# Depthwise convolutions: from 31 taps on GpSimd to block-diagonal products on TensorE

## The chip, the cores and the metric

The kernel runs on one core of a Trainium2 chip. The core has five engines that work at the same time, each through its own queue of instructions: TensorE (PE: matrix products; its weight loads are listed as PEld), VectorE (DVE), ScalarE (ACT), GpSimd (POOL) and SyncE (SP), which here only issues transfers (DMAs). The metric is the time of one execution on the device, in microseconds (us). Products write to PSUM, everything else lies in SBUF, 128 partitions each; weights and inputs come from DRAM.

## The reference, cut to what matters

Two blocks follow each other on one sequence of 256 tokens of 1024 features. The first is a state-space mixer with a squared-ReLU network. The second has two layers with two streams, the tokens x and a context ctx of 256 tokens. In each layer a stream is normalised, multiplied by w_in and split into parts for four branches (Fourier, convolution, grouped attention, differential attention), whose gated sum is multiplied by w_out; a SwiGLU network follows. In the second layer the context only gives keys and values. The branch that matters here:

```python
def conformer_conv(z, w, bias, ln_g, ln_b):          # z [256 tokens, 1024]
    a, g = jnp.split(z, 2, axis=-1)
    u = a * jax.nn.sigmoid(g)                          # [256, 512]
    pad = CONV_KERNEL // 2                             # 15; CONV_KERNEL = 31
    y = lax.conv_general_dilated(u, w[:, None, :].astype(u.dtype), window_strides=(1,),
                                 padding=[(pad, pad)], dimension_numbers=("NWC", "WIO", "NWC"),
                                 feature_group_count=CONV_WIDTH_2) + bias
    return jax.nn.silu(layer_norm(y, ln_g, ln_b))

def mixer_stream(parts, lp, cos, sin, ctx_kv, lam, lam_init):
    zf, zconv, zgq, zgk, zgv, zdq, zdk, zdv, zgate = parts
    y_four = fourier_mix(zf) @ lp["w_four"]
    y_conv = conformer_conv(zconv, lp["conv_w"], lp["conv_b"], ...) @ lp["w_conv"]
    ...                                                # the two attentions
    ys = jnp.stack([y_four, y_conv, y_gqa, y_diff], axis=2)
    return jnp.sum(gates * ys, axis=2) @ lp["w_out"]
```

Every one of the 512 channels has its own 31 taps, so y at token t is the sum over i of w[i] times u at token t + i - 15. It is computed three times: for ctx and x in layer 0, and for x in layer 1.

## The kernel before, in words

Activations lie as [features on partitions, 256 tokens], in chunks of 128 features. A large product is made in three passes of a rounded 32-bit type: weight and activation are each split into a high part and the rest, and high times high, high times rest and rest times high are summed (mm3, L337; token-major products do the same at L992 to L994). A weight unit of 512 KB is loaded by SP's queue into a ring of three buffers (ws), rounded by ScalarE (wh, L315) and its rest taken by VectorE (wl, L316), each into a ring of four. So a product waits for a load, ScalarE and VectorE in turn, and loads wait in SP's one queue, in order.

A convolution call (conv_start, L1417) has two parts. conv_in (L998) makes four chunks of 128 channels: two weight units, 48 products, a tanh on ScalarE (L1009) and a product on VectorE (L1010) that writes 2u into up, [128, 4, 286], with 15 zeros on each side of the tokens. conv_taps (L1013) works on GpSimd alone: for a chunk, tap 0 times up and the bias, then 30 times a multiplication into ct (L1025) and an addition to cy (L1026), each of 128x256. cy is read only much later, by conv_steps (L1029: layer norm and silu), beside the last gated branches. The three calls stand at L1653 (ctx, layer 0, inside the end of block 1), L1665 (x, layer 0) and L1693 (x, layer 1).

What follows a call on TensorE are the token-major products of keys, values and queries (w_tok), with their rotations on VectorE and their transposes (L1205), the attentions (softmax at L1249 to L1254; transposes at L1262; values) with Fourier and gated branches between their steps, and then the rest of the branches. RMS norms sum squares (ssq, L413), add over partitions on TensorE (L388), take 1/sqrt on VectorE by steps on columns of one or two elements (L366 to L381) and spread the row by a diagonal matrix dg (L396) and a product (L397).

The order on each engine is set when the program is built, by a scheduler that follows priorities (the order of the code, with shifts) and the rings of buffers: tiles of one tag and lane share as many buffers as BUFS gives, and a new tile waits for the last reader of an old one. The tag px of the main lane, small results in PSUM, has two. Modulation vectors are made in block 1 by float32 products with a stationary of 128x32, four of them on the four groups of 32 output rows (L902).

Of the kernel before, what the change touches and what calls it, by code (L numbers as in the profile page):

```python
# [9 lines left out]
F32 = mybir.dt.float32  # L10
# [7 lines left out]
P = 128  # L18
D = 1024
L = 256  # L20
# [7 lines left out]
# columns of the packed per-feature vector array  # L28
# [3 lines left out]
def _vec_layout():  # L32
    off = 0
    for name, n in (
        ("norm_ffn", 8), ("norm_ple", 8), ("norm_final", 8), ("final_norm", 8),
        ("norm_mix2", 16), ("norm_ffn2", 16), ("b_ada", 96), ("c", 16),
        ("conv_b", 8), ("ln_g", 8), ("ln_b", 8), ("diff_norm", 2), ("conv_w", 248),
        ("lam", 512), ("qn", 128), ("kn", 128),
    ):
        VEC[name] = (off, n)  # L40
        off += n
    return off
# [21 lines left out]
# ---------------------------------------------------------------- host layout  # L64
# [4 lines left out]
def _wfeat(w, cols_per_unit=1):  # L69
    """[K, M] -> [M/128 blocks][128, K/128, 128]."""  # L70
    k, m = w.shape
    return w.reshape(k // P, P, m // P, P).transpose(2, 1, 0, 3)


def host_layout(i):
# [5 lines left out]
    # rows (s, h), columns (g, c); token = 8c + s  # L81
# [22 lines left out]
    put("conv_w", a["conv_w_2"].reshape(2, 31, 4, P).transpose(3, 0, 2, 1).reshape(P, 248))  # L104
    lam = np.stack([a["lam_q1_2"], a["lam_k1_2"], a["lam_q2_2"], a["lam_k2_2"]], axis=1)
    put("lam", np.broadcast_to(lam.reshape(1, 512), (P, 512)))
# [10 lines left out]
    # group g = (half*4 + g4)*8 + j ; rows (half, p), columns (j, g4)  # L117
# [10 lines left out]
    # rows (re/im, p), columns (half, j, g4, h); then the same with re and im exchanged  # L128
# [12 lines left out]
    # block 1 weights  # L141
# [11 lines left out]
    # block 2 weights  # L153
    w_in = a["w_in_2"]
    # [l, 2048 columns, half, k] of [128, 4 * 256]: a quarter's columns side by side
# [5 lines left out]
    o["w_cin"] = np.stack(wc).reshape(8, P, 2048)  # L161
    tok = np.concatenate([w_in[:, :, 0:512], w_in[:, :, 1536:3840]], axis=2)
# [17 lines left out]
    for l in range(2):  # L180
        w = _wfeat(a["w_ffn2_2"][l])  # [8, 128, 22, 128]
# [7 lines left out]
    # constants of the shapes  # L189
# [18 lines left out]
    rope = np.stack([np.cos(ra), np.sin(ra)], axis=1)  # [256, 2, 32]  # L208
# [10 lines left out]
# ---------------------------------------------------------------- device side  # L219
class Act:  # L220
    """A [features, tokens] activation as hi/lo float32r tiles of 4 KB per partition."""
# [21 lines left out]
    def pair(self, k):  # L243
        """hi and lo of chunks k, k + 1 (both in one tile)."""
        i = k % self.per
        return self._tile(0, k)[:, i : i + 2, :], self._tile(1, k)[:, i : i + 2, :]


# buffers per tag and lane: m main, a attention and modulation vectors, c convolution, g gates
# [13 lines left out]
class Net:  # L263
# [7 lines left out]
    # ---- tiles  # L271
# [5 lines left out]
    def lane(self, s):  # L277
        """Tiles of one lane take turns among themselves, so lanes can run past each other."""
# [34 lines left out]
    # ---- hi/lo parts: hi is rounded to float32r, lo is the exact remainder  # L313
# [4 lines left out]
    def split_scaled(self, hi, lo, src, c):  # L318
        """hi + lo = c * src, c a constant or a column."""
# [3 lines left out]
    # ---- weights  # L323
    def wunits(self, ap, sizes=(1024, 1024)):
        """Load one weight chunk; return its units as (hi, lo) pairs."""
# [11 lines left out]
    def mm3(self, out, unit, act, ks, off=0, start=True, stop=True, cols=None):  # L337
        """out += unit[:, off + 128*i].T @ act[:, k] over ks, in three float32r passes."""
# [12 lines left out]
    def mm3x(self, outs, units, act, n=KC):  # L351
        """Several units over n chunks of act, chunk by chunk as act comes."""
# [7 lines left out]
    # ---- norms  # L360
    def newton(self, v, n):
        """1/sqrt(v) for v > 0, v in SBUF, [128, n]."""
# [21 lines left out]
    def colsum(self, out, ssq):  # L384
        """Sum of the tiles [128, 256] over partitions; the tokens land on the partitions of out [128, 2]."""
# [5 lines left out]
    def bcast(self, y):  # L391
        """[128 tok, 2] -> PSUM [128, 256]: the row of tokens on every partition."""
# [7 lines left out]
    def ssq_add(self, ssq, src, k, n, scale=None, eng=None):  # L400
        """Squares of chunk k of n: the last two stay apart, to be summed by colsum."""
# [17 lines left out]
    # ------------------------------------------------------------ S5  # L419
    def exp_small(self, out, x, n):  # L420
        """exp on a small [128, n] tile with float32 accuracy."""
# [58 lines left out]
    def s5_params(self):  # L480
# [21 lines left out]
        # powers a^(8-i), i = 0..7, [128, 32, 8]  # L502
# [17 lines left out]
        # coef = (a - 1) / lam  # L520
# [15 lines left out]
        # B-bar [128, ri, 32, 16]  # L536
# [12 lines left out]
        # rows (ri, p), columns (half, g): B-bar, zeros, B-bar; and the powers signed for C  # L549
# [13 lines left out]
        # recursion multipliers: [a^8 re | a^8 re], [-a^8 im | a^8 im]  # L563
# [7 lines left out]
    def b_outer(self, dst, g0, xr, xi):  # L571
        """dst[:, g, ri, i, h] = a[g]^(8 - i) * B[g, h]."""
# [15 lines left out]
    def s5(self):  # L588
# [12 lines left out]
        # normalised input, rows (s, h), columns (g, c)  # L601
# [18 lines left out]
        # chunk summaries S = sum_s a^(8-s) B u  # L620
# [7 lines left out]
        for jp in range(4):  # L628
            ss_sb = self.k4([P, 2, 2, 2, 64], F32, "ss")  # (j, ri, half, p) on rows (g4, c)
            for jj in range(2):  # L630
# [3 lines left out]
                pmt = self.k4([P, 4, 2, P], F32, "pmt")  # rows (s, h); (g4, ri, (half, p))  # L634
# [21 lines left out]
        # recursion over chunks  # L656
        for s in range(1, 31):
# [7 lines left out]
            if s in (23, 30):  # L665
                # from rows (half, p), columns (ri, g) to rows (ri, p), columns (half, g)
# [7 lines left out]
        # rows (ri, p): C a^s, minus the imaginary part; order i = 7 - s  # L674
# [9 lines left out]
        # taps K_tau = Re(C a^tau B), order i = 7 - tau; rows (g4, 2, h'), the second half one tap on  # L684
        for half in range(2):
# [15 lines left out]
            # intra-chunk matrices: rows (s', h'), columns (7 - s, h)  # L701
# [10 lines left out]
        # outputs, rows (g4, c); columns (7 - s, j, h)  # L712
# [40 lines left out]
    def c_outer(self, c, g0, c1, c2):  # L753
# [6 lines left out]
        # C conj-signed: re = Cr pr - Ci pi; -im = -Ci pr - Cr pi  # L760
# [6 lines left out]
    # ------------------------------------------------------------ block 1 after the mixer  # L767
    def ple_proj(self):
        """p @ ple_w, two tiles of four feature chunks."""
# [13 lines left out]
    def block1(self, ya, pe, early, fill):  # L783
        V, G, S, T, nc = self.V, self.G, self.S, self.T, self.nc
        x = self.x
        # gated linear unit, residual, first norm
# [20 lines left out]
        # squared-relu network; the row scale 1/rms enters squared, on its output  # L807
# [42 lines left out]
        # gated addition of p; the final norm and the next block's first norm  # L850
# [30 lines left out]
    # ------------------------------------------------------------ modulation vectors  # L881
    def silu_c(self):
        """silu of c and c_ctx as [128, k, 32] stationary columns, zero beyond the two."""
# [9 lines left out]
    def ada_steps(self, g):  # L893
        """Layer 0: modulation columns of 2048 features, silu(c) W, a quarter of them on each 32 rows."""
# [24 lines left out]
    def ada_late(self):  # L919
        """Layer 1: the products on the vector engine, their sums over the partitions on the tensor engine;  # L920
        each 32 rows carry 512 features of one of the two streams."""
# [30 lines left out]
    def ada_next(self, n=1):  # L952
        """Some steps of the modulation vectors left, beside other work."""
# [4 lines left out]
    def mod_gain(self, l, kind, norm):  # L958
        """norm * (1 + scale) as columns [128, 8, 2]."""
# [21 lines left out]
    # ------------------------------------------------------------ mixers  # L981
    def tok_seg(self, h, units):
        """[128 tok, 2, 256] = h[:, token blocks].T @ W from token-major weight units of four k;
        a generator, one step per token block."""
# [13 lines left out]
    def conv_in(self, l, h):  # L998
        V, S, G = self.V, self.S, self.G
        up = self.up.tile([P, 4, L + 30], F32, tag="up", name=self.nm("up"))  # L1000
        G.memset(up[:, :, 0:15], 0.0)
        G.memset(up[:, :, L + 15 : L + 30], 0.0)
# [732 lines left out]
```

## Time and profile before

| | |
|---|---|
| runs of the kernel | 2120.98, 2123.73 and 2126.22 us, median 2123.73 |
| profiled execution, span from first to last instruction | 2118.8 us |
| TensorE busy | 1945.7 us, 92% of the span |
| VectorE busy | 1582.7 us, 75% |
| ScalarE busy | 928.6 us, 44% |
| GpSimd busy | 773.5 us, 37% |

The time of an execution is the span and a little around it, which the profile doesn't list; the span shown stands 4.9 us under the median. The profile is one execution. A group of instructions is told by its line, engine and operation, then out<-in by the program's names and the shapes; "busy, mean ns of one" and the idle time of the engine before them follow. A window's row gives the busy time and number of instructions of PE, PEld, DVE, ACT and POOL, in this order, in a stretch, and the granted clock of TensorE as a share of full speed. A mean over the span hides that stages have different limits, so the rows further down go by stretch.

### The profile page before, as it was taken

Reading aid. Unit: us, or ns where it says so; the run is one execution under the profiler, and the core shown is the slowest. Engines: PE = TensorE matmul, PEld = TensorE weight load, DVE = VectorE, ACT = ScalarE, POOL = GpSimd, SP = SyncE. Lnnn points to the kernel's source line nnn. Section 1 sums busy time; section 2 is a strip of 40 time slices with the busy share of each in tenths; the row PEclk is TensorE's granted clock in tenths of the full one; section 3 lists DMA queues with packets and bytes.
Section 4 is the critical chain, followed back from the end, with each engine's and each line's share of the span. In section 5 each row is a group of like instructions: output and inputs, shape, how many; then the busy total and the mean of one; then the engine's idle time right before and its main releaser. Section 6 shows DMA issues by size and latency. Waiting matters only on the chain. (4 is left out here: it accounts for less than half of the span.)

```text
span 2118.8 us, 39621 instructions
## 1 busy us (share of the span) xinstructions
PE 1945.7 (92%) x15666; PEld 1811.3 (85%) x15666; DVE 1582.7 (75%) x2761; ACT 928.6 (44%) x1583; POOL 773.5 (37%) x882
## 2 busy tenths in 40 slices
PE   3869999986999997898999999999997899999998
PEld 1457999985789996777999989989997778999997
DVE  9974686779687779879868766675769887766665
ACT  2443444543654554553554222222454554554443
POOL 6620000199980039999000000000139997000000
PEclk9989999998999998999999999999998999999999
DMA  5566665542245563224563445443553224554553
GB/s 186 166 229 222 214 204 185 173 139 80 88 134 165 181 198 100 79 70 150 187 201 131 159 149 163 156 159 118 151 178 103 68 75 135 180 196 157 185 188 112
DMA packets 102920, 323.70 MB, mean 153 GB/s; under 512 B 16384, under 2 KB 18320, under 8 KB 102352
## 3 DMA queue, kind: packets, MB, share of 16 engines
q1 hardware_dynamic: 101968, 319.53, 46.5%
q8 instruction: 123, 2.02, 0.4%
q0 software_dynamic: 336, 1.44, 0.2%
q14 instruction: 61, 0.50, 0.1%
q10 hardware_dynamic: 432, 0.21, 0.0%
HBM read 317.47 MB, written 1.05 MB: 150 GB/s over the span
## 5 line engine op out<-in xcount | busy, mean ns | idle before, releaser
L316 DVE TENSOR_TENSOR wl<-ws,wh 128x1024 fp32r<-128x1024 f32 (+3 forms) x556 | 660.5, 1198 | 314.2 <-ACT wh L315 309.5
L315 ACT CAST wh<-ws 128x1024 fp32r<-128x1024 f32 (+3 forms) x556 | 531.9, 959 | 742.5 <-PE pm L348 415.9
L413 POOL TENSOR_TENSOR ssq<-ssq,sq 128x256 f32<-128x256 f32 x45 | 43.7, 972 | 1203.8 <-ACT sq L407 1202.3
L347 PE MATMUL pm<-h,wh 128*128 128x256 f32 x1264 | 357.6, 283 | 0.0
L349 PE MATMUL pm<-h,wl 128*128 128x256 f32 x1264 | 355.2, 281 | 0.0
L348 PE MATMUL pm<-h,wh 128*128 128x256 f32 x1264 | 355.1, 281 | 0.0
L1026 POOL TENSOR_TENSOR cy<-cy,ct 128x256 f32<-128x256 f32 x360 | 337.7, 938 | 0.1
L1025 POOL TENSOR_TENSOR ct<-up,vecs 128x256 f32<-128x256 f32 x360 | 316.8, 881 | 0.0
L347 PEld LDWEIGHTS pm<-h,wh 128*128 128x128 f32 x1264 | 240.5, 190 | 8.4 <-issue 5.8
L348 PEld LDWEIGHTS pm<-h,wh 128*128 128x128 f32 x1264 | 240.8, 190 | 1.7 <-issue 1.7
L349 PEld LDWEIGHTS pm<-h,wl 128*128 128x128 f32 x1264 | 239.1, 189 | 0.0
L347 PE MATMUL pm<-m,wh 128*128 128x256 f32 (+1 forms) x704 | 213.7, 304 | 0.0
L348 PE MATMUL pm<-m,wh 128*128 128x256 f32 (+1 forms) x704 | 213.2, 303 | 0.1
L349 PE MATMUL pm<-m,wl 128*128 128x256 f32 (+1 forms) x704 | 212.6, 302 | 0.0
L347 PE MATMUL pm<-hx,wh 128*128 128x256 f32 x640 | 184.8, 289 | 0.0
L349 PE MATMUL pm<-hx,wl 128*128 128x256 f32 x640 | 180.9, 283 | 1.0 <-DVE wl L316 1.0
L348 PE MATMUL pm<-hx,wh 128*128 128x256 f32 x640 | 180.8, 282 | 0.0
L347 PEld LDWEIGHTS pm<-m,wh 128*128 128x128 f32 x704 | 134.1, 191 | 8.4 <-PE pm L349 1.7
L936 DVE SCALAR_TENSOR_TENSOR ac<-wa,sc,ac 128x512 f32<-128x512 f32 x168 | 119.3, 767 | 28.0 <-DMA wa<-w_ada 28.0
L348 PEld LDWEIGHTS pm<-m,wh 128*128 128x128 f32 x704 | 134.2, 191 | 6.7 <-issue 1.7
L349 PEld LDWEIGHTS pm<-m,wl 128*128 128x128 f32 x704 | 134.1, 191 | 4.9
L347 PEld LDWEIGHTS pm<-hx,wh 128*128 128x128 f32 x640 | 121.5, 190 | 2.2 <-issue 2.0
(429 smaller groups left out, 4867.9 us busy)
## 6 DMA issues: line engine op xcount, KB each, us to landing
wa<-w_ada SPq DMA_DIRECT2D x96, 512.0 KB, 3.9
ws<-w_gp SPq DMA_DIRECT2D x96, 512.0 KB, 3.6
ws<-w_f SPq DMA_DIRECT2D x88, 512.0 KB, 4.1
ws<-w_tok SPq DMA_DIRECT2D x76, 512.0 KB, 3.9
ws<-mlp_w SPq DMA_DIRECT2D x64, 512.0 KB, 4.2
ws<-w_gp SPq DMA_DIRECT2D x96, 256.0 KB, 2.7
ws<-w_f2a SPq DMA_DIRECT2D x32, 512.0 KB, 4.4
ws<-w_cin SPq DMA_DIRECT2D x24, 512.0 KB, 4.6
```

Of the source, the lines that this page charges most:

```text
L315: self.S.copy(hi, src)
L316: self.V.tensor_tensor(lo, src, hi.bitcast(F32), op=ALU.subtract)
L347: self.T.matmul(out, h, ah, start=start and i == 0, stop=False)
L348: self.T.matmul(out, h, al, start=False, stop=False)
L349: self.pe_last = self.T.matmul(out, l, ah, start=False, stop=stop and i == n - 1)
L413: (eng or self.G).tensor_tensor(acc, acc, sq, op=ALU.add)
L936: V.scalar_tensor_tensor(acc[:, v], st[:, i], c, acc[:, v], op0=ALU.mult, op1=ALU.add)
L1025: G.tensor_tensor(t, up[:, k, i : i + L], wb[i], op=ALU.mult)
L1026: G.tensor_tensor(y[:, k], y[:, k], t, op=ALU.add)
```

## The change

The taps leave GpSimd. For each chunk k of 128 channels, up is now a tile [128, 288] of its own (two buffers). It is copied to a scratch in DRAM (du, two buffers), and four transfers copy it back into ux, [128, 4, 284], of which there is one buffer: rows 32i to 32i+31 of ux hold, for each q of 4, the 32 channels 32q to 32q+31, shifted by i tokens. A matrix cw, [128, 8, 4, 32], comes from a new array w_cv made on the host: for j of 8 and q of 4 its row 32i + c has in column c the tap 4j + i of channel 32q + c, and zeros elsewhere (tap 31 is zero). 32 float32 products with a 128x32 stationary then make the chunk: product (j, q) adds four taps for 32 channels onto PSUM rows 32q to 32q+31, from ux shifted by 4j tokens. ScalarE adds the bias into cy.

The taps and the vectors of the differential attention's lambda leave the array of per-feature vectors, which has 458 columns in place of 1218; lambda_col loads its 256 columns itself. Comments and docstrings are removed as well, which shifts line numbers: L347 to L349 become L352 to L354, L992 to L994 become L997 to L999, L1205 becomes L1211.

```diff
-    def conv_in(self, l, h):
-        V, S, G = self.V, self.S, self.G
-        up = self.up.tile([P, 4, L + 30], F32, tag="up", name=self.nm("up"))
-        G.memset(up[:, :, 0:15], 0.0)
-        G.memset(up[:, :, L + 15 : L + 30], 0.0)
+    def conv_start(self, l, h):
+        V, S, G, T = self.V, self.S, self.G, self.T
+        y = self.k4([P, 4, L], F32, "cy")
         for k in range(4):
             ua, ug = self.wunits(self.a["w_cin"][l * 4 + k])
             ps = self.pm((P, 2, L))
             self.mm3(ps[:, 0], ug, h, range(KC))
             self.mm3(ps[:, 1], ua, h, range(KC))
+            up = self.up.tile([P, CW], F32, tag="up", bufs=2, name=self.nm("up"))
+            G.memset(up[:, 0:15], 0.0)
+            G.memset(up[:, L + 15 : CW], 0.0)
             t = self.k1([P, L])
             S.activation(t, ps[:, 0], AF.Tanh, scale=0.5)
-            V.scalar_tensor_tensor(up[:, k, 15 : 15 + L], t, 1.0, ps[:, 1], op0=ALU.add, op1=ALU.mult)
-        return up
-
-    def conv_taps(self, l, up):
-        G = self.G
-        y = self.k4([P, 4, L], F32, "cy")
-        with self.lane("c"):
-            for k in range(4):
-                w = self.vec("conv_w", (l * 4 + k) * 31, 31)
-                wb = [w[:, i : i + 1].to_broadcast([P, L]) for i in range(31)]
-                G.tensor_tensor(y[:, k], up[:, k, 0:L], wb[0], op=ALU.mult)
-                G.tensor_tensor(y[:, k], y[:, k], self.cb2[:, l * 4 + k : l * 4 + k + 1].to_broadcast([P, L]), op=ALU.add)
-                for i in range(1, 31):
-                    t = self.k1([P, L], F32, "ct")
-                    G.tensor_tensor(t, up[:, k, i : i + L], wb[i], op=ALU.mult)
-                    G.tensor_tensor(y[:, k], y[:, k], t, op=ALU.add)
+            V.scalar_tensor_tensor(up[:, 15 : 15 + L], t, 1.0, ps[:, 1], op0=ALU.add, op1=ALU.mult)
+            out = self.dr.tile([P, CW], F32, tag="du", name=self.nm("du"))
+            self.nc.sync.dma_start(out, up)
+            sh = self.up.tile([P, 4, L + 28], F32, tag="ux", name=self.nm("ux"))
+            v = out.rearrange("(q c) s -> c q s", c=32)
+            for i in range(4):
+                self.nc.sync.dma_start(sh[32 * i : 32 * i + 32], v[:, :, i : i + L + 28])
+            w = self.k4([P, 8, 4, 32], F32, "cw")
+            self.nc.sync.dma_start(w.rearrange("p j q c -> p (j q c)"), self.a["w_cv"][l * 4 + k])
+            ps = self.px()
+            for j in range(8):
+                for q in range(4):
+                    T.matmul(ps[32 * q : 32 * q + 32, :], w[:, j, q], sh[:, q, 4 * j : 4 * j + L],
+                             start=j == 0, stop=j == 7)
+            S.activation(y[:, k], ps, AF.Identity, bias=self.cb2[:, l * 4 + k : l * 4 + k + 1])
         return y
...
+        lam = self.k1([P, 4, 64], F32, "lam")
+        self.nc.sync.dma_start(lam.rearrange("p a b -> p (a b)"), self.a["lam"][:, l * 256 : l * 256 + 256])
...
+            self.dr = pool("dr", 2, space=bass.MemoryType.DRAM)
...
+    cw = np.concatenate([a["conv_w_2"], np.zeros((2, 1, 512), np.float32)], axis=1).reshape(2, 8, 4, 4, 4, 32)
+    cv = np.zeros((2, 4, 4, 32, 8, 4, 32), np.float32)
+    e = np.arange(32)
+    cv[:, :, :, e, :, :, e] = cw.transpose(5, 0, 3, 2, 1, 4)
+    o["w_cv"] = cv.reshape(8, P, 1024)
```

On TensorE, in layer 0 of the x stream, the first transposes of keys (L1205, from w) stand after the third group of token-major products (into pm) in the kernel before:

```order
L992 MATMUL pm_10088<-wh_10084,hx_9297 128x256
L993 MATMUL pm_10088<-wh_10084,hx_9299 128x256
L994 MATMUL pm_10088<-wl_10085,hx_9297 128x256
L1205 MATMUL px_10167<-identr,w_10164 128x128 x4
L1205 MATMUL px_10181<-identr,w_10178 128x128 x4
L992 MATMUL pm_10201<-wh_10191,hx_9072 128x256
```

In the changed kernel the same transposes stand at L1211, and the products of the fourth chunk's convolution (L1030, from ux and cw) before them:

```order
L997 MATMUL pm_10097<-wh_10087,hx_8891 128x256
L998 MATMUL pm_10097<-wh_10087,hx_8893 128x256
L1030 MATMUL px_9545<-ux_9538,cw_9543 32x256 x32
L1211 MATMUL px_9799<-identr,w_9796 128x128 x4
L999 MATMUL pm_10097<-wl_10088,hx_8891 128x256
L997 MATMUL pm_10097<-wh_10087,hx_8891 128x256
L1211 MATMUL px_9813<-identr,w_9810 128x128 x4
L998 MATMUL pm_10097<-wh_10087,hx_8893 128x256
```

The transposes moved behind two more groups of products, apart from each other by three dense products, and take px buffers after the convolution's.

On SP, at the same place in the program, the queue before holds weight loads alone (ws from w_cin for the convolution's input, from w_tok for the keys, values and queries):

```order
L329 DMA ws_9514<-w_cin 128x1024
L329 DMA ws_9520<-w_cin 128x1024
L329 DMA ws_9947<-w_tok 128x1024
L329 DMA ws_9953<-w_tok 128x1024
L329 DMA ws_10014<-w_tok 128x1024
```

In the changed kernel the copies stand between them: du out to DRAM, ux back in four parts, cw with the taps:

```order
L334 DMA ws_9475<-w_cin 128x1024
L334 DMA ws_9579<-w_tok 128x1024
L1020 DMA du_9206<-up_9200 128x288
L334 DMA ws_9585<-w_tok 128x1024
L1024 DMA ux_9208<-du_9206 32x4x284 x4
L1020 DMA du_9316<-up_9310 128x288
L1020 DMA du_9426<-up_9420 128x288
L334 DMA ws_9646<-w_tok 128x1024
L334 DMA ws_9652<-w_tok 128x1024
L334 DMA ws_9708<-w_tok 128x1024
L1024 DMA ux_9318<-du_9316 32x4x284 x4
L1026 DMA cw_9323<-w_cv 128x1024
```

The second chunk's ux (ux_9318) stands behind three weight loads of w_tok and takes the one ux buffer after the first chunk's products; weight loads behind it wait for its issue.

## Rows read from the trace of the kernel before

**Rows 1.** First line of the page.

```profile
span 2118.8 us, 39621 instructions
```

**Rows 2.** Windows: stretch, length, busy us (instructions) by engine, clock, DMA share, GB/s.

```profile
419.00:637.00 218.00, 185.21 (x1384) 171.60 (x1384) 176.81 (x328) 105.67 (x218) 211.07 (x250) 0.93 0.34 110
637.00:781.00 144.00, 144.00 (x1214) 143.78 (x1213) 107.06 (x196) 75.69 (x126) 5.53 (x5) 1.00 0.56 181
781.00:1020.00 239.00, 203.56 (x1516) 186.05 (x1516) 206.16 (x327) 112.58 (x210) 223.05 (x260) 0.95 0.35 111
795.00:848.00 53.00, 37.31 (x283) 35.97 (x282) 48.56 (x63) 21.03 (x35) 53.00 (x61) 0.87 0.30 100
1569.00:1805.00 236.00, 208.50 (x1565) 191.53 (x1564) 192.04 (x313) 115.02 (x213) 215.38 (x248) 0.95 0.34 105
```

**Rows 3.** Costliest groups of the page: the taps' additions.

```profile
L1026 POOL TENSOR_TENSOR cy<-cy,ct 128x256 f32<-128x256 f32 x360 | 337.7, 938 | 0.1
```

**Rows 4.** TensorE's waits, 419 to 637: us in total, times, longest.

```profile
PE px L397 <- DVE dg L396: 10.2, 3, 7.3
...
PE px L1262 <- DVE sm L1250: 5.3, 3, 4.3
```

**Rows 5.** TensorE's waits, 781 to 1020.

```profile
PE px L1262 <- DVE sm L1250: 8.8, 5, 4.6
```

**Rows 6.** TensorE's waits, 1569 to 1805.

```profile
PE px L1262 <- DVE sm L1250: 8.7, 5, 4.6
```

**Rows 7.** VectorE's timeline from 473.5: start, us, instruction, idle before it.

```profile
473.72 0.16 DVE L381 TENSOR_SCALAR sm<-px 128x2 f32<-128x2 f32 x1 [4.33 <-PE px L388]
...
479.25 1.71 DVE L316 TENSOR_TENSOR wl<-ws,wh 128x1024 fp32r<-128x1024 f32 x1
...
484.95 0.71 DVE L396 TENSOR_SCALAR dg<-ident,y 128x128 f32<-128x128 f32 x1
```

**Rows 8.** VectorE's timeline from 1909.5.

```profile
1912.33 0.15 DVE L381 TENSOR_SCALAR sm<-px 128x2 f32<-128x2 f32 x1
...
1914.23 0.48 DVE L396 TENSOR_SCALAR dg<-ident,y 128x128 f32<-128x128 f32 x2
```

**Rows 9.** VectorE's groups by form, 419 to 637.

```profile
L1249 DVE TENSOR_REDUCE sm<-px 128x1 f32<-128x256 f32 x32 | 13.0, 407 | 1.7 <-PE px L1313 1.7
...
L413 DVE TENSOR_TENSOR ssq<-ssq,sq 128x256 f32<-128x256 f32 x10 | 8.4, 891 | 0.0
L371 DVE SCALAR_TENSOR_TENSOR sm<-y,sm 128x1 f32<-128x1 f32 x12 | 7.5, 659 | 0.0
```

**Rows 10.** VectorE's groups by form, 637 to 781.

```profile
L371 DVE SCALAR_TENSOR_TENSOR sm<-y,sm 128x1 f32<-128x1 f32 x6 | 1.0, 216 | 0.0
...
L413 DVE TENSOR_TENSOR ssq<-ssq,sq 128x256 f32<-128x256 f32 x1 | 0.4, 423 | 0.0
```

**Rows 11.** TensorE's timeline from 157: L902 and a dense product.

```profile
157.52 0.64 PE L902 MATMUL px<-wa,sc 128*32 128x256 f32 x8
158.09 0.39 PE L347 MATMUL pm<-y,wh 128*128 128x256 f32 x1
158.40 0.62 PE L902 MATMUL px<-wa,sc 128*32 128x256 f32 x2
```

**Rows 12.** TensorE's timeline from 270.5.

```profile
270.90 0.28 PE L349 MATMUL pm<-h,wl 128*128 128x256 f32 x1
271.11 1.50 PE L902 MATMUL px<-wa,sc 128*32 128x256 f32 x24
272.55 0.39 PE L347 MATMUL pm<-h,wh 128*128 128x256 f32 x1
272.77 0.28 PE L348 MATMUL pm<-h,wh 128*128 128x256 f32 x1
```

**Rows 13.** DMA issues of the page: count, KB each, us to landing.

```profile
ws<-w_tok SPq DMA_DIRECT2D x76, 512.0 KB, 3.9
...
mt<-kt SPq DMA_DIRECT2D x7, 128.0 KB, 3.7
```

More of the change, by code (lines that the diff above doesn't have):

```diff
@@ L36, in _vec_layout @@
         ("norm_mix2", 16), ("norm_ffn2", 16), ("b_ada", 96), ("c", 16),
-        ("conv_b", 8), ("ln_g", 8), ("ln_b", 8), ("diff_norm", 2), ("conv_w", 248),
-        ("lam", 512), ("qn", 128), ("kn", 128),
+        ("conv_b", 8), ("ln_g", 8), ("ln_b", 8), ("diff_norm", 2),
+        ("qn", 128), ("kn", 128),
     ):
@@ L103, in host_layout @@
     put("diff_norm", a["diff_norm_2"].T)
-    put("conv_w", a["conv_w_2"].reshape(2, 31, 4, P).transpose(3, 0, 2, 1).reshape(P, 248))
     lam = np.stack([a["lam_q1_2"], a["lam_k1_2"], a["lam_q2_2"], a["lam_k2_2"]], axis=1)
-    put("lam", np.broadcast_to(lam.reshape(1, 512), (P, 512)))
+    o["lam"] = np.broadcast_to(lam.reshape(1, 512), (P, 512))
     put("qn", np.broadcast_to(a["q_norm_2"].reshape(1, 128), (P, 128)))
@@ L1359, in lambda_col @@
             t, s = self.sm([P, 64]), self.sm([P, 1])
-            V.tensor_tensor(t, self.vec("lam", (l * 4 + 2 * i) * 64, 64), self.vec("lam", (l * 4 + 2 * i + 1) * 64, 64), op=ALU.mult)
+            V.tensor_tensor(t, lam[:, 2 * i], lam[:, 2 * i + 1], op=ALU.mult)
             V.tensor_reduce(s, t, op=ALU.add, axis=AX.X)
@@ L1415, in behind @@
         return self.tc.issue_after(self.pe_last.ins)
-    def conv_start(self, l, h):
-        return self.conv_taps(l, self.conv_in(l, h))
     def mixer(self, l, st, x, h, rope, cy, ckv, nlam, hook):
@@ L1711 @@
 NH = 6
+CW = L + 32
 ADA_OFF = 50
```

## Prediction

> **What bounds the kernel now.** I read the page's first rows for the span, then its costliest groups for what the change takes away, then windows of the engines, then the waits and the timelines inside them.
>
> The span is 2118.8 us [rows 1], 4.9 below the median of the three runs, 2123.73; I take the profiled execution for one like them and add 4.9 to every span, so each sum below starts at 2123.7. The taps are 720 instructions on POOL, half of them the additions at L1026, 0.94 each [rows 3]. They lie in three stretches, one for each call: 419 to 637 (context stream, layer 0), 781 to 1020 (x, layer 0) and 1569 to 1805 (x, layer 1). In each POOL is busy over nine tenths of the time, and in each TensorE is not: it stands idle 218.0 - 185.2 = 32.8, 239.0 - 203.6 = 35.4 and 236.0 - 208.5 = 27.5 us, 95.7 together [rows 2]. In the stretch between the first two POOL has nearly nothing to do, and TensorE is busy all of it, 1214 products in 144.0 us, 0.119 each. [...] So 95.7 + 28 = 124 us in which TensorE loses time lie in the stretches with taps. The kernel is bound by TensorE outside them, and by short chains on VectorE inside them.
>
> That the chains are long because of the taps is the step on which all hangs. One RMS norm's row of factors (L381 to L396) takes VectorE 473.72 to 485.66, 11.9 us, beside the taps [rows 7], and TensorE waits 7.3 us for its end, L396 [rows 4]. The same chain at 1912.33, without POOL, takes 2.4 [rows 8]. By form: L371, 128x1 with two operands in SBUF, is 659 ns beside taps and 216 in the stretch between; L413, 128x256, 891 and 423 [rows 9, 10]. L1249, 256 columns read from PSUM, stays at 407 in the middle of the taps [rows 9], no longer than an L413 alone.
>
> **The change part by part.**
>
> Taken away: the taps, and with them that lengthening. How much of the 124 us stays? The chain shown gives one end, 2.4 / 11.9 = 0.2. Between its pieces stand two L316 of about 1.71 which the free chain doesn't have; counted in full, (2.4 + 3.4) / 11.9 = 0.5 is the other end [rows 7, 8]. Third, TensorE's waits for the softmax (L1262 on L1250) are 5.3, 8.8 and 8.7 us [rows 4 to 6]; the maximum there is L1249, which the taps don't lengthen, so I expect most of these 22.8 to stay, 0.24 of the idle. I take 0.3 for idle time and clock alike: it keeps 29 and 8 and gives back 87.
>
> [...]
>
> Added on TensorE: 12 chunks of 32 float32 products, eight times four, each four on the four groups of 32 columns. The same shape (128x32 stationary, 256 moving) stands in the trace as L902. One set of four goes from 157.52 to the next product at 158.09, 0.57 [rows 11]; three sets from 271.11 to 272.55, 1.44 [rows 12]. So a further set costs (1.44 - 0.57) / 2 = 0.435. What lies around: from L349 at 270.90 to the second product behind it, 272.77, are 1.87; two dense products would have been 0.24; so three sets added 1.63, of which 1.305 are the sets and 0.33 the entry and the way back. Eight sets: 0.33 + 8 x 0.435 = 3.8 us; twelve chunks: 45.7. It is all on the path, since TensorE is what the kernel waits for once the chains are short. The lower end is 8 x 0.435 x 12 = 41.8 (gaps hidden where TensorE waits anyway). The upper end is that sets don't overlap at all, a rival below.
>
> [...]
>
> Moved on TensorE: a convolution's products stand in a fixed place in its order. In the x stream the four stand 75 to 88 dense products apart, 9 to 10.5 us at 0.119, the first some 130 behind its chunk's last product, and the fourth just before the first transpose of keys. Behind a late copy everything on TensorE waits. The way to it: tanh, L1010, du out, four parts of ux back, the latter two after the product before, since ux has one buffer. For a part of ux I take the 3.7 us of mt<-kt, 128 KB [rows 13], the four beside each other as they go out in a row; that is 5 us inside the 9. A wait of nothing, then. Two transposes of keys now share two px buffers with the fourth convolution and wait for ScalarE's copy of it, about 1 us in each of three calls: 3 us.
>
> Moved on SP: 12 du, 48 parts of ux and 12 cw of 512 KB between the weight loads, which are in one queue with them. A ux that waits for TensorE holds back the ws behind it. A ws needs 3.9 us to land [rows 13] and about 2.5 for its rounding and its rest; the orders put the products that use it some 100 and more behind, 12 us. So they are covered, as long as no du or ux waits over 5 us. They carry 6 MB of cw and 9 MB of copies in 690 us, 22 GB/s beside some 110, where a third of the DMA engines' time is used [rows 2].
>
> ScalarE gets 12 Identity of 256 columns and VectorE nothing; both have gaps in all three stretches [rows 2]. The vector array is 380 KB shorter and lam comes by two loads at the start: 0, within 1 us either way.
>
> Sum: 2123.7 - 87 + 45.7 + 3 = 2086 us. By ends: a kept share of 0.2 with the lower price, 2123.7 - 99 + 42 + 0 = 2067; of 0.5 with the higher, 2123.7 - 62 + 49 = 2111.
>
> **The rivals.**
>
> The idle time is the chains' own. Taps and attention lie in the same stretches, so the windows alone cannot part them: what TensorE waits for may be steps in a row, whatever each takes. For it: L1249 is not lengthened, and the softmax waits are there in all three. Against it: the norm's chain, five times longer beside taps, and 7.3 of its time seen as a wait. With 0.55 to 0.75 kept the time is 2123.7 - (56 to 31) + 48.7 = 2117 to 2141; over 0.6 the change pays nothing.
>
> The copies hold TensorE (slower). Single place: ux's one buffer. The four parts are issued only after the last convolution's products and must all land before the next, 9 to 10.5 us later. If they go one after another, 4 x 3.7 = 14.8, or stand behind three ws loads, 3 x 3.9 + 3.7 = 15.4 [rows 13], TensorE waits 4.5 to 5.5 us at nine places (the first of each call has 15), 40 to 50, and lets the clock fall. It decides from a landing over 10 us on. Time: 2086 + 40 to 50 = 2126 to 2136. Against it: the issues come in one row, and 16 engines a third busy take them.
>
> The sets don't overlap. One L902 by itself (two records, as each leaves) takes 0.62 [rows 11]; 384 x 0.62 = 238, so 2123.7 - 87 + 238 + 3 = 2278. For it nothing but the doubt whether L902's sets, whose four products share a stationary, stand for a stationary that changes with each.
>
> All the idle time goes, 0 to 0.1 kept: 2049 to 2061. The dense stretch between shows that such a density can be held, but it has no attention in it.
>
> **How the numbers follow.** Forecast (kept 0.1 to 0.5) 0.69, 2061 to 2111; all idle goes 0.07; chains' own 0.13; copies hold 0.07; no overlap 0.04. The likeliest is 2086. The range 2055 to 2126 leaves out half of the case with all idle gone, the upper half of the chains' own, most of the copies and the sets: about 0.19. A run of this kernel tells a change of 0.3%, 6.4 us, from none. Faster than 2117.4: 0.69 + 0.07 + 0.01 = 0.77. Within 6.4: 0.06 of the chains' own and 0.01 of the copies, 0.07. Slower than 2130: 0.06 + 0.06 + 0.04 = 0.16.
>
> **What the changed profile would show.** POOL's busy time falls by the taps, 720 x 0.9 = some 650 us. In the first stretch L371 falls to about 216 and L413 to 423; if they don't, the taps weren't the cause. TensorE's idle time in the three stretches falls from 95.7 to about 29 and the granted clock rises to 0.98; if the softmax waits (L1262) are larger than 22.8, the rival of the chains is right. A group of 32 products at L1030 takes 3.5 to 3.8 us; near 20 it is the sets. Waits of TensorE for DMA ux, or of SP's later weight loads that end in a wait for wl, would be the copies. I am wrong if the time is over 2111 with the convolutions at their price, since then the kept share is not what the norm's chain says.

## The result and the profile after

The changed kernel takes 2031.7 us (2030.4 to 2032.3) against 2122.6 of the kernel before, timed beside it: 0.957 of its time, interval 0.956 to 0.959, 91 us less. The forecast was 2086, 38 less, with a range from 2055; the time lies below the range. The direction, the cause and nearly the price of the new products were right; what comes back was more than forecast.

The page of the changed kernel, first line and busy times by engine, for [rows 1]:

```profile
span 2028.5 us, 40563 instructions
...
PE 1950.7 (96%) x16434; PEld 1806.2 (89%) x16434; DVE 1419.1 (70%) x2761; ACT 929.4 (46%) x1595; POOL 127.8 (6%) x156
```

GpSimd is busy 646 us less, as the taps would have it, and VectorE 164 us less with the same 2761 instructions. The three stretches that had the taps, found by about the same work in the changed trace; the columns are those of [rows 2]:

```profile
419.40:608.40 189.00, 188.45 (x1632) 170.74 (x1631) 122.07 (x324) 105.47 (x222) 0.64 (x8) 0.99 0.48 150
752.00:957.00 205.00, 204.66 (x1775) 184.93 (x1774) 147.66 (x325) 113.72 (x214) 5.12 (x18) 1.00 0.48 152
1507.60:1714.00 206.40, 205.94 (x1788) 186.12 (x1788) 137.70 (x309) 113.37 (x215) 0.32 (x4) 1.00 0.45 139
```

TensorE's idle time in them is 189.0 - 188.45, 205.0 - 204.66 and 206.4 - 205.94, together 1.4 us, where it was 95.7. The granted clock is 0.99 to 1.00. The stretches are 29, 34 and 30 us shorter, although TensorE does four convolutions more in each. The longest of TensorE's waits in the first, where [rows 4] had 10.2 and 5.3:

```profile
PE px L1268 <- DVE p L1288: 0.4, 1, 0.4
```

VectorE's groups by form, 419.4 to 620, for [rows 9] (L1255, L418 and L376 are L1249, L413 and L371 before):

```profile
L321 DVE TENSOR_TENSOR wl<-ws,wh 128x1024 fp32r<-128x1024 f32 x44 | 53.5, 1222 | 41.9 <-ACT wh L320 41.9
L1255 DVE TENSOR_REDUCE sm<-px 128x1 f32<-128x256 f32 x32 | 13.1, 410 | 2.5 <-PE px L1319 2.0 <-PE px L1286 0.4
L418 DVE TENSOR_TENSOR ssq<-ssq,sq 128x256 f32<-128x256 f32 x10 | 3.9, 424 | 2.2 <-ACT sq L412 2.2
L376 DVE SCALAR_TENSOR_TENSOR sm<-y,sm 128x1 f32<-128x1 f32 x12 | 2.1, 212 | 0.0
```

L418 falls from 891 to 424 ns and L376 from 659 to 212, which are the numbers of the quiet stretch [rows 10]; the reduction is 407 before and 410 now. TensorE's timeline at the first convolution, for [rows 11, 12]:

```profile
433.19 0.28 PE L352 MATMUL pm<-hc,wh 128*128 128x256 f32 x1
433.40 3.66 PE L1030 MATMUL px<-ux,cw 128*32 128x256 f32 x64
436.99 0.38 PE L353 MATMUL pm<-hc,wh 128*128 128x256 f32 x1
437.21 0.28 PE L354 MATMUL pm<-hc,wl 128*128 128x256 f32 x1
```

From the dense product at 433.19 to the second one behind the group are 4.02 us; two dense products take 0.24, so the group added 3.8, as forecast. The DMA issues (count, KB each, us to landing), for [rows 13]:

```profile
ux<-du SPq DMA_DIRECT2D x48, 142.0 KB, 4.0
cw<-w_cv SPq DMA_DIRECT2D x12, 512.0 KB, 6.4
du<-up SPq DMA_DIRECT2D x12, 144.0 KB, 3.9
```

The four parts of ux, issued one behind another in 1.8 us at the first chunk, land beside each other, each in 4.0 in the median, and no wait of TensorE for ux or cw is in the list.

### The profile page after: what moved, and what is told of

The parts are those of the page before. It is cut to its first block, busy times and chain, and to the rows that moved or that the text cites. A ratio compares the mean times of both kernels' runs of the same rounds, so it can differ in the third digit from the quotient of the medians.

```text
span 2028.5 us, 40563 instructions
## 1 busy us (share of the span) xinstructions
PE 1950.7 (96%) x16434; PEld 1806.2 (89%) x16434; DVE 1419.1 (70%) x2761; ACT 929.4 (46%) x1595; POOL 127.8 (6%) x156
## 5 line engine op out<-in xcount | busy, mean ns | idle before, releaser
L321 DVE TENSOR_TENSOR wl<-ws,wh 128x1024 fp32r<-128x1024 f32 (+3 forms) x556 | 615.0, 1115 | 372.4 <-ACT wh L320 367.8
L352 PE MATMUL pm<-h,wh 128*128 128x256 f32 x1264 | 357.7, 283 | 0.0
L354 PE MATMUL pm<-h,wl 128*128 128x256 f32 x1264 | 354.7, 281 | 0.0
L352 PEld LDWEIGHTS pm<-h,wh 128*128 128x128 f32 x1264 | 238.6, 189 | 8.4 <-issue 5.0
L354 PEld LDWEIGHTS pm<-h,wl 128*128 128x128 f32 x1264 | 240.0, 190 | 0.0
L352 PE MATMUL pm<-m,wh 128*128 128x256 f32 (+1 forms) x704 | 213.7, 304 | 0.0
L354 PE MATMUL pm<-m,wl 128*128 128x256 f32 (+1 forms) x704 | 212.6, 302 | 0.0
L352 PE MATMUL pm<-hx,wh 128*128 128x256 f32 x640 | 182.2, 285 | 0.0
L353 PE MATMUL pm<-hx,wh 128*128 128x256 f32 x640 | 178.6, 279 | 0.0
L354 PE MATMUL pm<-hx,wl 128*128 128x256 f32 x640 | 178.1, 278 | 0.0
L418 POOL TENSOR_TENSOR ssq<-ssq,sq 128x256 f32<-128x256 f32 x45 | 43.7, 971 | 1669.9 <-ACT sq L412 1668.4
L352 PEld LDWEIGHTS pm<-m,wh 128*128 128x128 f32 x704 | 134.4, 191 | 8.4 <-PE pm L354 1.7
L354 PEld LDWEIGHTS pm<-m,wl 128*128 128x128 f32 x704 | 134.5, 191 | 4.9
L352 PEld LDWEIGHTS pm<-hx,wh 128*128 128x128 f32 x640 | 121.2, 189 | 2.2 <-issue 2.0
L353 PEld LDWEIGHTS pm<-hx,wh 128*128 128x128 f32 x640 | 121.2, 189 | 1.0 <-issue 0.8
L354 PEld LDWEIGHTS pm<-hx,wl 128*128 128x128 f32 x640 | 121.1, 189 | 0.0
```

Source lines behind the costliest of these rows:

```text
L321: self.V.tensor_tensor(lo, src, hi.bitcast(F32), op=ALU.subtract)
L352: self.T.matmul(out, h, ah, start=start and i == 0, stop=False)
L353: self.T.matmul(out, h, al, start=False, stop=False)
L354: self.pe_last = self.T.matmul(out, l, ah, start=False, stop=stop and i == n - 1)
L418: (eng or self.G).tensor_tensor(acc, acc, sq, op=ALU.add)
```

## The experiments

The two traces leave two readings. In the first, called contention in what was expected, the taps lengthened VectorE's instructions, this was the whole loss, and the new products are a pure price. In the second, called cover, part of the idle time belonged to the chains, and the new products filled it, so that their price was partly paid by waits.

**No taps beyond the first.** The kernel before with tap 0 and the bias on GpSimd; taps 1 to 30 are left out, and it is called the kernel without taps below.

```diff
-                for i in range(1, 31):
+                for i in range(1, 1):
```

> The kernel before with tap 0 and the bias alone on GpSimd; taps 1 to 30 are left out of the convolution, nothing is added on TensorE. Contention (the taps' reads lengthen VectorE's instructions, and that alone makes TensorE idle and its clock fall): the idle time (96 us) and the clock (39 us, counted from the two traces) go, 2122.6 - 135 = 1988 us, 1982 to 1996. Cover (part of the idle time belongs to the chains, and in the changed kernel the convolutions' products filled it): without those products some 15 us or more stay idle, 2003 or more.

Measured: 1989.6 us, ratio 0.937 (0.936 to 0.939), 133.7 less than before. Windows of TensorE and the rest in three stretches without the taps:

```profile
419.00:608.00 189.00, 188.46 (x1509) 177.28 (x1507) 133.29 (x350) 111.93 (x231) 5.08 (x10) 1.00 0.41 138
737.00:927.00 190.00, 189.00 (x1508) 176.31 (x1507) 145.95 (x323) 111.20 (x210) 11.61 (x20) 1.00 0.41 137
1480.00:1680.00 200.00, 199.53 (x1596) 186.46 (x1595) 141.89 (x316) 115.85 (x216) 4.60 (x8) 1.00 0.38 127
```

TensorE is busy without the new products too: 2.0 us idle in 579. There was nothing left for them to fill. Cover falls, and the price of the whole new path is 2031.7 - 1989.6 = 42.1 us (39.1 by the second timing of the changed kernel, 2028.7, further down).

**Both.** The changed kernel, with as many instructions of the taps' kind beside it.

```diff
+            if k == 0:
+                up0 = up
...
+            if k == 0:
+                self.taps(up0)
...
+    def taps(self, up):
+        w = [self.vec("b_ada", i).to_broadcast([P, L]) for i in range(31)]
+        with self.lane("c"):
+            d = self.k1([P, L], F32, "cd")
+            self.G.tensor_tensor(d, up[:, 0:L], w[0], op=ALU.mult)
+            for i in range(120):
+                t = self.k1([P, L], F32, "ct")
+                self.G.tensor_tensor(t, d, w[1 + i % 30], op=ALU.mult)
+                e = self.k1([P, L], F32, "cd")
+                self.G.tensor_tensor(e, d, t, op=ALU.add)
+                d = e
```

> The changed kernel, and beside it 241 multiplications and additions of 128x256 on GpSimd per call, started by the first chunk, whose result is not used. Contention: the lengthening comes back in full, 2031.7 + 120 to 140 = 2152 to 2172 us. Cover: the convolutions' products fill the waits that the lengthening makes, so the time is near that of the kernel before, 2115 to 2140.

Measured: 2149.3 us, 1.012 of the kernel before (1.010 to 1.014) and 118 more than the changed kernel. Its first stretch:

```profile
419.00:653.00 234.00, 209.87 (x1706) 188.86 (x1705) 168.20 (x336) 110.50 (x230) 208.21 (x249) 0.93 0.39 126
```

24 us idle and a clock of 0.93 are back, with the convolutions' products in the stretch. 118 of 134 is most of it, 3 short of the range expected. The lengthening did not come back in full either: VectorE is busy 1542.1 us, 123 more than in the changed kernel, where the taps before cost it 165 (1582.7 against 1417.6 without them), and L418 takes 728 ns, not 891. So the rest of the 134 needs no cover; whether some of it is the other order is not settled.

**Only writes.** Taps 1 to 30 replaced by memsets, so that GpSimd is as busy and reads nothing.

```diff
-                for i in range(1, 31):
-                    t = self.k1([P, L], F32, "ct")
-                    G.tensor_tensor(t, up[:, k, i : i + L], wb[i], op=ALU.mult)
-                    G.tensor_tensor(y[:, k], y[:, k], t, op=ALU.add)
+                for i in range(60):
+                    G.memset(y, 0.5)
```

> The kernel before with taps 1 to 30 replaced by 60 memsets per chunk of 128x1024 on GpSimd, at the 0.955 us that such a memset takes in the trace, so GpSimd is as busy as before and reads nothing; taps 1 to 30 are left out of the convolution. If it is GpSimd's reads of SBUF that lengthen VectorE: as without taps, 1988 us, 1982 to 1998. If any work of GpSimd's does: near 2122, over 2090. Between them if writes lengthen it in part.

Measured: 2098.6 us, over the 2090 of the second reading, but it decides nothing. The waits from 419 to 2000 (us, times, longest), two of TensorE's and one of VectorE's, name a fault of the experiment:

```profile
PE pm L347 <- DVE k L1384: 43.7, 2, 26.8
PE px L1038 <- DVE m L1034: 16.3, 1, 16.3
```

```profile
DVE m L1032 <- POOL cy L1024: 55.1, 3, 24.5
```

L1032 to L1034 add up the chunks of cy for the layer norm. The memsets (L1024) ended after L1032 wanted the tile, three times, once for each convolution call. So with 48:

> The kernel before with taps 1 to 30 replaced by 48 memsets per chunk of 128x1024 on GpSimd (60 before, which ended after the layer norm wanted their tile); 30 of 31 taps are left out. In the stretches the 60 cost 5 to 8 us each against the kernel without taps, and three late ends some 90. If only that is so: 1989.6 + 3 x 6 = 2008 us, 2000 to 2016. If writes lengthen VectorE as reads do: 2070 or more.

Measured: 2016.4 us, 26.8 more than without taps, where the reading taps cost 133.7; GpSimd was busy with memsets for 559 us. The result is 0.4 over the range of the first expectation and far under the 2070 of the second. VectorE's groups by form, 419 to 600, with 48 memsets:

```profile
L316 DVE TENSOR_TENSOR wl<-ws,wh 128x1024 fp32r<-128x1024 f32 x42 | 51.3, 1221 | 26.2 <-ACT wh L315 26.0
...
L1280 DVE TENSOR_SCALAR p<-p,sm 128x256 f32<-128x256 f32 x16 | 10.3, 646 | 0.1
...
L413 DVE TENSOR_TENSOR ssq<-ssq,sq 128x256 f32<-128x256 f32 x10 | 3.6, 418 | 0.0
...
L1248 DVE TENSOR_SCALAR sm<-sm,qn 128x1 f32<-128x1 f32 x16 | 3.2, 202 | 0.1
...
L371 DVE SCALAR_TENSOR_TENSOR sm<-y,sm 128x1 f32<-128x1 f32 x12 | 2.0, 209 | 0.0
```

And the tensor_scalar of L1280 (L1282 there) in the kernel without taps, then in the kernel before, beside the taps (419 to 637):

```profile
L1282 DVE TENSOR_SCALAR p<-p,sm 128x256 f32<-128x256 f32 x16 | 5.5, 347 | 0.1
```

```profile
L1282 DVE TENSOR_SCALAR p<-p,sm 128x256 f32<-128x256 f32 x16 | 8.8, 549 | 0.1
```

Beside the memsets L413 and L371, with two operands in SBUF, keep their free times (418 and 209 ns; 417 and 213 without taps, 891 and 659 beside them), while the tensor_scalar of 128x256 goes from 347 to 646; the one of 128x1 (L1248) takes 202, and 208 without taps. The taps, which read and write, lengthen L413, L371 and this tensor_scalar too (549). So in these shapes it depends on what GpSimd does which instructions are lengthened; why it does was not shown.

**Half the taps.**

```diff
-                for i in range(1, 31):
+                for i in range(1, 16):
```

> The kernel before with taps 0 to 15 and the bias on GpSimd; 15 of 31 taps are left out, so GpSimd works half as long in each stretch, its first half. If every tap costs the same, half of the 133.6 us between the kernel without taps (1989.6) and the kernel before: 2056 us, 2049 to 2063. If it matters which chains lie beside them: against the kernel without taps, the kernel before had lost 36 of 43 us by the middle of the first stretch, 28 of 48 in the second and some 29 of 39 in the third, so 93 in all, 2083, 2074 to 2092.

Measured: 2086.6 us. Half the taps cost 97 of the 133.7. The result is in the range of the second expectation, which was worked out from where the loss lies in the stretches. So the loss is not in proportion to the number of taps. That it goes by what stands beside them (the first half of each stretch has the norms, the rotations of keys and the first scores, whose ends TensorE waits for) fits this; a run with only the later taps was not made.

**One set of eight.** This was meant to price the products.

```diff
-            for j in range(8):
+            for j in range(1):
...
-                             start=j == 0, stop=j == 7)
+                             start=j == 0, stop=True)
```

> The changed kernel with only the first of the eight sets of four products per chunk; 28 of 32 taps are left out of the convolution, all copies stay. Contention: the products are a pure price, 84 sets x 0.435 = 36.5 us less than 2031.7, 1995 us, 1990 to 2000. Cover: taking them out opens idle time, 2005 to 2031.

Measured: 2039.3 us, 8 more than with eight sets, against both expectations. TensorE's largest waits, 419 to 2000:

```profile
PE px L1030 <- DMA ux<-du: 15.0, 3, 5.7
PE pm L997 <- ACT wh L320: 7.7, 4, 3.2
PE pm L352 <- ACT wh L320: 5.5, 2, 3.1
```

The order on TensorE had changed. In the x stream of layer 0 the second and third convolutions stand with no product between them:

```order
L1030 MATMUL px_9185<-ux_9178,cw_9183 32x256 x4
L1030 MATMUL px_9267<-ux_9260,cw_9265 32x256 x4
```

The second of them waits for ux, whose one buffer the first has only just given back, and the weight loads on SP stand behind that ux. So it prices nothing, but it shows the rival of the copies at work: TensorE waits for ux, 15.0 us in three waits. In the changed kernel 75 to 88 dense products stand there, and no such wait is listed.

**Every product twice.** The price, with the distances kept.

```diff
-            for j in range(8):
+            for n in range(16):
+                j = n % 8
...
-                             start=j == 0, stop=j == 7)
+                             start=n == 0, stop=n == 15)
```

> The changed kernel with every product of the convolutions made twice into the same sum (the convolution comes out doubled before its bias). If the products are a pure price of 0.435 a set, 12 x 8 x 0.435 = 41.8 us more than 2031.7: 2073.5, 2070 to 2078. If their first half is partly hidden in waits, the second half costs more than the first did against the kernel without taps (42.1 us from 1989.6 to 2031.7), over 2080; if TensorE still had gaps to give, less, under 2068.

Measured: 2068.7 us, 37.0 more than the changed kernel, between the 2070 of a pure price and the 2068 of gaps. One group in its timeline:

```profile
432.59 7.11 PE L1031 MATMUL px<-ux,cw 128*32 128x256 f32 x128
```

7.11 - 3.66 = 3.45 for eight more sets, 0.431 each, or 41.4 for all twelve groups. The run shows 4 us less than that. Against the second timing of the changed kernel, 2028.7 (further down), it is 40.0, so most of the 4 us lie between two timings of the changed kernel. A first half that was partly hidden would have made it over 2080, and it didn't.

**The copies on GpSimd's queue.** GpSimd is free now, and SP holds weight loads.

```diff
-            self.nc.sync.dma_start(out, up)
+            G.dma_start(out, up)
...
-                self.nc.sync.dma_start(sh[32 * i : 32 * i + 32], v[:, :, i : i + L + 28])
+                G.dma_start(sh[32 * i : 32 * i + 32], v[:, :, i : i + L + 28])
...
-            self.nc.sync.dma_start(w.rearrange("p j q c -> p (j q c)"), self.a["w_cv"][l * 4 + k])
+            G.dma_start(w.rearrange("p j q c -> p (j q c)"), self.a["w_cv"][l * 4 + k])
```

> The changed kernel with du, ux and cw issued by GpSimd's queue in place of SP's. If the copies hold back weight loads on SP (they stand between them), up to 5 us less than 2031.7. If neither queue is on the path, the same within 2 us. If GpSimd's issues land later, so that TensorE waits for ux, 2036 or more.

Measured: 2041.6 us, 10 more. In the median of its twelve transfers du lands later, 5.9 against 3.9, and TensorE waits for ux:

```profile
du<-up POOLq DMA_DIRECT2D x12, 144.0 KB, 5.9
```

```profile
PE px L1030 <- DMA ux<-du: 9.6, 2, 5.1
```

The two waits are at the first chunk of the second and the third call. There the four parts of ux took 6.7 and 6.3 us from issue to landing in the median, where they took 3.7 and 3.0 at the same places in the changed kernel. So it is ux more than du that is late there, by some 3 us, and the hidden copies become waits of 5.1 and 4.5: the margin of the changed kernel is small. Why ux lands later at these two and not in the median of all 48 (3.8 against 4.0) is not settled.

**Parts in bfloat16.** A cheaper product, for a version better than both. du and ux hold the two parts in bfloat16, so that eight transfers bring back a chunk in place of four.

```diff
-            up = self.up.tile([P, CW], F32, tag="up", bufs=2, name=self.nm("up"))
+            up = self.up.tile([P, 2, CW], BF16, tag="up", bufs=2, name=self.nm("up"))
...
-            V.scalar_tensor_tensor(up[:, 15 : 15 + L], t, 1.0, ps[:, 1], op0=ALU.add, op1=ALU.mult)
+            V.scalar_tensor_tensor(t, t, 1.0, ps[:, 1], op0=ALU.add, op1=ALU.mult)
+            S.copy(up[:, 0, 15 : 15 + L], t)
+            V.tensor_tensor(up[:, 1, 15 : 15 + L], t, up[:, 0, 15 : 15 + L], op=ALU.subtract)
...
+            wb = self.k4([P, 2, 8, 4, 32], BF16, "cb")
+            S.copy(wb[:, 0], w)
+            V.tensor_tensor(wb[:, 1], w, wb[:, 0], op=ALU.subtract)
...
+                for n, (u, b) in enumerate(((0, 0), (0, 1), (1, 0))):
+                    for q in range(4):
+                        T.matmul(ps[32 * q : 32 * q + 32, :], wb[:, u, j, q], sh[:, b, q, 4 * j : 4 * j + L],
+                                 start=j == 0 and n == 0, stop=j == 7 and n == 2)
```

> The changed kernel with the convolution's products in bfloat16: its input and its taps each as a high part and the rest, three products in place of one float32 product (high x high, high x rest, rest x high). A float32 set of four took 0.435; three bfloat16 sets of four at about 0.119 each (the spacing of dense products of 256 columns) take 0.357, so 96 x (0.435 - 0.357) = 7.5 us less: 2024, 2018 to 2030. If sets of four bfloat16 products don't overlap, 12 x 96 products at 0.119 = 137 in place of 42: about 2127. If the splitting of input and taps on ScalarE and VectorE delays the copies past the products' place, 2035 or more.

Measured: 2023.6 us (2020.5 to 2029.1). A part of a group in its timeline:

```profile
434.01 2.70 PE L1038 MATMUL px<-ux,cb 128*32 128x256 bf16 x92
```

92 products are 23 sets of four, 0.117 each, where one dense product of 256 columns takes 0.119: they overlap, as the float32 sets do. Since 8 us is little between two timings made apart, both once more, side by side:

> The changed kernel once more, beside the one with bfloat16 parts on the same chip: 2031.7, 2029 to 2034.

> The kernel with bfloat16 parts beside the changed one: a set of three bfloat16 products costs less than a float32 set, 0.36 against 0.435, and its group of 96 products lasted about 2.9 us in place of 3.66, so 12 x 0.75 = 9 us less than the changed kernel of the same call, 6 to 11. If the gain of the first time was the chip's or chance, within 3.

Measured: 2028.7 for the changed kernel (0.956, 0.954 to 0.958) and 2023.8 for the other (0.954, 0.953 to 0.956), 4.9 us apart, less than the 6 to 11 expected. Part of the saving goes where a group is split around dense products and pays its entry again; one set by itself takes 0.22, from 434.78 to 435.00, against 0.117 within a group (the second timing's trace):

```profile
434.78 0.29 PE L1038 MATMUL px<-ux,cb 128*32 128x256 bf16 x4
435.00 0.38 PE L353 MATMUL pm<-g,wh 128*128 128x256 f32 x1
```

It is the lowest time of the kernels that do all the work, by 0.2%; the intervals of the two against the kernel before overlap.

## Why the prediction was wrong

**What comes back: the step that failed.** The prediction kept 0.3 of idle time and lost clock and gave back 87 us. Without taps 133.7 come back. Of the idle time 1.4 of 95.7 us stay in the changed kernel, 0.01. This is 47 of the 54 us by which the forecast missed: 37 are the 0.3 of 124 that was kept, and 10 lie in the clock below and in the spread of the timings. Of the rest, 7 are in the price below and 1 in the start of the sum (2123.7 for 2122.6).

The kept share was taken from the lengths of a chain, 2.4 of 11.9 us at one end. But a wait is only what is left of a chain after the products that TensorE has beside it. In the wait of 7.3 us of [rows 4], the chain starts at 473.72 [rows 7], and TensorE has products until 478.48:

```profile
478.20 0.28 PE L993 MATMUL pm<-wh,hc 128*128 128x256 f32 x1
485.81 0.77 PE L397 MATMUL px<-dg,ones 128*128 128x128 f32 x2 [7.34 <-DVE dg L396]
```

So 4.8 of the 11.9 us were covered, and the rest was the wait. The same chain in the changed kernel, first step, a weight's rest within it, and first dg:

```profile
479.09 0.16 DVE L386 TENSOR_SCALAR sm<-px 128x2 f32<-128x2 f32 x1 [1.79 <-PE px L393]
...
479.89 1.23 DVE L321 TENSOR_TENSOR wl<-ws,wh 128x1024 fp32r<-128x1024 f32 x1
...
482.08 0.29 DVE L401 TENSOR_SCALAR dg<-ident,y 128x128 f32<-128x128 f32 x1
```

It takes 3.3 us, 0.28 of its length before: the ratio of lengths was well guessed. But 3.3 is less than 4.8, so nothing of the wait stays: TensorE takes up the product from dg (L402) at 485.99 without one, and no wait for L401 is listed in the three stretches. One of the two weight rests that made the other end, 0.5, is still there and holds nothing up.

The third ground of the prediction misread the trace. It said that the softmax waits, L1262 on L1250, belong to the chain, because the reduction L1249 in it is not lengthened. But the wait of 4.61 us that is the longest of [rows 5] ends like this (TensorE's timeline before, then VectorE's):

```profile
845.19 1.08 PE L1262 MATMUL px<-ident,p 128*128 128x128 f32 x4 [4.61 <-DVE sm L1250]
```

```profile
837.98 0.66 DVE L373 TENSOR_TENSOR sm<-y 128x16 f32<-128x16 f32 x1
838.68 0.54 DVE L374 TENSOR_TENSOR sm<-sm,sm 128x16 f32<-128x16 f32 x1
...
841.08 0.54 DVE L376 SCALAR_TENSOR_TENSOR y<-sm,y 128x16 f32<-128x16 f32 x1
841.65 0.65 DVE L1169 COPY qn<-y 128x16 f32<-128x16 f32 x1
842.33 0.21 DVE L1250 TENSOR_SCALAR sm<-sm,qn 128x1 f32<-128x1 f32 x1
843.48 0.16 DVE L1254 RECIPROCAL sm<-sm 128x1 f32<-128x1 f32 x1 [0.94 <-ACT p L1252]
...
844.15 0.90 DVE L1282 TENSOR_SCALAR p<-p,sm 128x512 f32<-128x512 f32 x1
844.97 0.20 DVE L1250 TENSOR_SCALAR sm<-sm,qn 128x1 f32<-128x1 f32 x1
```

The first L1250 stands behind the steps of the head norms, L373 to L376, at 0.54 to 0.70 each; the same steps in the changed kernel:

```profile
797.50 0.17 DVE L379 TENSOR_TENSOR sm<-sm,sm 128x16 f32<-128x16 f32 x1
797.71 0.17 DVE L381 SCALAR_TENSOR_TENSOR y<-sm,y 128x16 f32<-128x16 f32 x1
```

From 837.98 to the end of the wait VectorE had one gap, 0.94 us. L1250, which ends the wait, had its own length (0.20), but it was late by its queue, and the L1282 ahead of it, which belongs to the softmax, was lengthened too (0.90; the mean of this shape is 764 ns in [rows 5]'s stretch and 480 in the changed kernel). In the kernel without taps, which has no new products either, this is all that TensorE's waits from 419 to 2000 list for the softmax's transposes, where the prediction counted 22.8:

```profile
PE px L1262 <- DVE p L1282: 0.2, 1, 0.2
```

The 0.24 of the idle time that the prediction counted for these waits falls with them.

**The clock.** The sum has 28 us of lost clock; no run shows this term. The trace before shows a fall of the clock at the wait of 7.3 us of [rows 4], which ends at 485.81: the granted clock is 0.50 from 484 to 489, where dense products stand 0.21 apart (488.00 and 488.21), and 1.00 from 490 to 491, where they stand 0.12 apart. For the whole loss the runs show this: from the profiled execution before to the one without taps, TensorE is idle 94.8 us less, and it is busy 33.8 us less with the same 15666 records (1945.7 and 1911.9). So the clock, with time between products that the profile counts as busy, is 34 here, between the 28 and the 39 of the expectation for the kernel without taps. How the two split is not settled.

**The price** was forecast at 48.7: 3.8 a group by the rows, 45.7 in all, and an estimate of 3 for the px buffers. Measured are 42.1 for the whole path, or 39.1 by the second timing. A group did add 3.8; where the path comes out cheaper than twelve of them is not settled. The 3 were not seen: no wait of that kind is in the list. The row of the same shape told the price of a set: 0.435 by it and 0.431 in the doubled groups.

**The copies** stayed off the path, as forecast, and for the reason given, the distance in TensorE's order. That the case is near shows in the waits with one set of eight, 15.0 us, and with GpSimd's queue, 9.6.

**The rivals.** All idle time gone was the right one; it had 0.07, at 2049 to 2061. Its own sum was short by the clock term and the price. That the waits are the chains' own, at 0.13, is refuted by the kernel without taps.

## What to carry to other kernels

When a second engine slows VectorE's instructions, don't scale a wait by how much shorter its chain becomes. Take from the shorter chain what the waiting engine has to do beside it; what is left is the new wait, and it can be nothing (here a chain of 3.3 us beside 4.8 us of products). Ask also of each wait whether VectorE was behind at that moment, not only whether the instruction that ends the wait is longer: if there are no gaps ahead of it, the wait belongs to the backlog and goes with it. The loss need not follow the amount of work: here half of the taps cost 97 of 133.7 us. A copy that is hidden only by distance in another engine's order should be known by its margin, since any change of the order or of the queue can use it up.

## What the runs showed of the hardware

GpSimd's writes alone lengthen VectorE's tensor_scalar of 128x256 (347 to 646 ns), not the one of 128x1 (202), and leave L413 and L371, with two operands in SBUF, alone (418 and 209 ns). Taps that read as well lengthen those (424 to 891 and 212 to 659). The reduction of 256 columns from PSUM (L1249) is not lengthened by the taps (407 and 410). Sets of four products on the four groups of 32 columns overlap also where each has its own stationary: 0.431 us for four in float32 with 256 columns, where one L902 by itself keeps the next product back by 0.55 (158.40 to 158.95 [rows 11]), and 0.117 for four in bfloat16, where one dense product takes 0.119. Issued by GpSimd's queue, du landed 2 us later in the median (5.9 against 3.9).
